# Four blocks of a depthwise convolution as ScalarE products and GpSimd sums, in place of three blocks as diagonal products on TensorE

## The chip, the cores and the metric

The kernel runs on one core of one Trainium2 chip. The metric is device microseconds of one execution, and the time given for a kernel is the median of its runs. Five engines take part: TensorE (PE in the rows, its weight loads PEld), VectorE (DVE), ScalarE (ACT), GpSimd (POOL) and SyncE (SP), which issues most DMAs. Each has its own queue of instructions, works through it in order, and waits on semaphores for the others.

## The reference, cut to what matters

Two transformer-like blocks over 256 tokens of width 2048 in float32. The first block starts with a mixer of two branches. One branch is a state-space model; the other is a convolution over time:

```python
def conformer_conv(a, w_dw, b_dw, ln_g, ln_b, w_pw):
    glu = a[..., :CONV_WIDTH] * jax.nn.sigmoid(a[..., CONV_WIDTH:])      # 1024 channels
    padded = jnp.pad(glu, ((0, 0), (CONV_KERNEL - 1, 0), (0, 0)))        # 31 taps
    y = lax.conv_general_dilated(padded, w_dw[:, None, :], ..., feature_group_count=CONV_WIDTH)
    y = y + b_dw
    y = jax.nn.silu(layernorm(y, ln_g, ln_b))
    return y @ w_pw
```

Every channel is convolved with its own 31 weights: y[c, t] = b[c] + sum over k of w[c, k] * glu[c, t + k - 30]. The rest of the model (the expert layer, a gated delta network and a banded attention) is not touched by the change.

## The kernel before

Activations lie with channels on the 128 partitions and the 256 tokens along the free axis, so 1024 channels are eight blocks of 128x256. A weight strip of 128x1024 float32 arrives by DMA (`raw`, line 150), ScalarE rounds it into a high part `wh` (line 162), VectorE subtracts to get the low part `wl` (line 163), and TensorE makes two products for each of its eight 128x128 pieces (`dual`, lines 175 and 176): the high part times the high and low halves of the activations (512 columns), the low part times the high half (256 columns). After 16 such pairs the two halves of the PSUM tile are folded together (ScalarE line 181, VectorE line 182), and VectorE scales the result into SBUF (`evict`, line 342).

While such products run, other work is woven between them. A `Side` holds generators; `mix` advances each of them by a fraction of a step after every pair, so a number in `STEP` is steps per block of 16 pairs. The instructions that a step traces on VectorE are held behind the last `wl` subtraction; what it traces on ScalarE and GpSimd is held by data, buffers and its place in the program alone. A scheduler fixes the order of each engine's queue when the kernel is built.

The convolution is made in the loop of line 415, which runs over the 32 blocks of the gates (blocks 24 to 55 of `w_in`) and in which three things are woven:

- `side`, the state-space scan, at 2 steps a block: VectorE products, additions and scans (lines 595 and 614 to 628), two GpSimd additions of 128x256 for every scan (lines 630 and 631), and TensorE products (lines 611, 612 and 639).
- `side2`, `conv` (line 665), blocks 0 to 4 of the convolution on VectorE, at 2.25 steps a block. A step is one tap of three blocks (0, 1, 2) and, after 31 steps, of two (3, 4): one `scalar_tensor_tensor` of 128x256 for each block and tap (line 674). That makes 62 steps.
- `side3`, `conv_pe` (line 704), blocks 5 to 7 on TensorE, at 3.7 steps a block. For each block, `glu` is split into high and low halves (line 722 on ScalarE, 723 on VectorE); for each tap ScalarE makes two 128x128 diagonal matrices from the identity (lines 728 and 729), in a ring of three, and TensorE multiplies with them by `dual`. After 31 taps the result is folded and moved to `cy` with its bias (line 718).

When `side3` has run out, the normalization `conv_norm` is put behind `conv` in the queue of `side2`. It sums all eight blocks of `cy` on TensorE (line 682). `glu`, `cy` and the weights `dw` are slices of the tile `cw`, and appear under that name in the rows.

Of the kernel before, what the change touches and what calls it, by code (L numbers as in the profile page):

```python
# [10 lines left out]
F32 = mybir.dt.float32  # L11
F32R = mybir.dt.float32r
# [4 lines left out]
AF = mybir.ActivationFunctionType  # L17
ALU = mybir.AluOpType
# [4 lines left out]
P = 128  # L23
W1 = 1024
W2 = 512
STEP = (6, 2, 2.25, 3.7, 3, 2)
GRATE = 0.2
DSTEP = 4.4
LAG = 7
# [8 lines left out]
GATE = 1024.0  # L38
GB = 8
GLAG = 2  # L40
CDVE = ((0, 1, 2), (3, 4))
CPE = (5, 6, 7)
DLAG = 2
TSTEP = 2
T = 256
KT = 16
# [70 lines left out]
class K:  # L117
# [189 lines left out]
    def mixers(self):  # L307
        nc, tc, I = self.nc, self.tc, self.I
        with ExitStack() as ctx:
            E = ctx.enter_context  # L310
            c1 = E(tc.tile_pool(name="c1", bufs=1))
# [5 lines left out]
            x = self.operand()  # L317
# [3 lines left out]
            o, w = VEC["mix"]  # L321
# [19 lines left out]
            def evict(dst, ps):  # L341
                nc.vector.tensor_tensor(out=dst, in0=ps, in1=rstd, op=ALU.mult)

            def block(n, between=None):
                ps = self.gemm([w_in[n, 0], w_in[n, 1]], x, between)
                return ps
# [34 lines left out]
            for j in range(3, 8):  # L381
                ps = block(16 + j, self.mix((side, STEP[5] / 16, "V")))
                evict(u[:, j, :], ps)

            glu = cw[:, 0:2288].rearrange("p (k t) -> p k t", k=8)
            cy = cw[:, 2304:4352].rearrange("p (k t) -> p k t", k=8)
            dw = cw[:, 4352:4600].rearrange("p (k t) -> p k t", k=8)
# [3 lines left out]
            for j in range(8):  # L391
                pa = block(j, self.mix((side, STEP[0] / 32, "V")))
                a = sm.tile([P, T], F32, name="ca")
                evict(a, pa)
                pg = block(8 + j, self.mix((side, STEP[0] / 32, "V")))
                g = sm.tile([P, T], F32, name="cg")
# [6 lines left out]
            side2 = Side()  # L403
            side2.add(self.conv(glu, cy, dw, CDVE))
            c4 = E(ExitStack())
            dg = c4.enter_context(tc.tile_pool(name="dg", bufs=DLAG + 1))
            side3 = Side()
            side3.add(self.conv_pe(c1, dg, glu, cy, dw, CPE))
            norm = self.conv_norm(sm, cy, *cx)
            bg = self.big_tile("bg")  # L410
            gt = bg.rearrange("p (k t) -> p k t", k=32)
# [3 lines left out]
            for j in range(32):  # L415
                ps = block(24 + j, self.mix((side, STEP[1] / 16, "V"), (side2, STEP[2] / 16, "V"), (side3, STEP[3] / 16, "V")))
                g = sm.tile([P, T], F32, name="gg")
# [11 lines left out]
            for j in range(16):  # L429
                ps = self.gemm([I["conv_w_out"][j, 0]], cx, self.mix((side, STEP[4] / 8, "V")))  # L430
                nc.vector.scalar_tensor_tensor(out=gt[:, j, :], in0=gt[:, j, :], scalar=1.0, in1=ps, op0=ALU.add, op1=ALU.mult)
# [33 lines left out]
            for j in range(16):  # L465
# [3 lines left out]
                ps = self.gemm([I["w_out"][j, 0], I["w_out"][j, 1]], mx)  # L469
# [231 lines left out]
            V.tensor_tensor(out=cl[:, j, :], in0=cy[:, j, :], in1=ch[:, j, :].bitcast(F32), op=ALU.subtract)  # L701
        yield

    def conv_pe(self, c1, dg, glu, cy, dw, js):

        nc = self.nc
        n = js[0]
        dh = c1.tile([P, len(js), 31], F32R, name="dwh")
        nc.scalar.copy(dh, dw[:, n:, :])
        dl = c1.tile([P, len(js), 31], F32, name="dwl")  # L710
        nc.vector.tensor_tensor(out=dl, in0=dw[:, n:, :], in1=dh.bitcast(F32), op=ALU.subtract)
        late = []

        def taps(ps, d, g, j, k):
            self.dual(ps, d[0], d[1], g[:, :, k : k + T], k == 0, k == 30)
            if k == 30:
                ps = self.fold(ps)
                nc.scalar.activation(cy[:, j, :], ps, AF.Identity, bias=self.vec("cb", j))

        for j in js:  # L720
            g = dg.tile([P, 2, 30 + T], F32R, name="g", bufs=1)
            nc.scalar.copy(g[:, 0], glu[:, j, :])
            nc.vector.tensor_tensor(out=g[:, 1], in0=glu[:, j, :], in1=g[:, 0].bitcast(F32), op=ALU.subtract)
            yield
            ps = self.ips.tile([P, 512], F32, name="cps", tag="i")
            for k in range(31):
                d = [dg.tile([P, P], F32R, name="d%d" % i) for i in range(2)]
                nc.scalar.activation(d[0], self.ident, AF.Copy, scale=dh.bitcast(F32)[:, j - n, k : k + 1])
                nc.scalar.activation(d[1], self.ident, AF.Copy, scale=dl[:, j - n, k : k + 1])
                late.append((ps, d, g, j, k))  # L730
                if len(late) > DLAG:
                    taps(*late.pop(0))
                yield
            while late:
                taps(*late.pop(0))
            yield


# [1027 lines left out]
```

## Time and profile before

| what | value |
|---|---|
| median of 3 runs | 3355.14 us (3352.12 to 3356.29) |
| the profiled execution | 3351.08 us |
| its span in the profile | 3349.3 us |
| mean granted clock of TensorE | 0.996 |
| TensorE busy | 3291.0 us (98%) |
| VectorE busy | 2667.1 us (80%) |
| ScalarE busy | 2021.3 us (60%) |
| GpSimd busy | 171.6 us (5%) |

Busy time is the union of the instructions' durations as recorded. A duration includes what the instruction waits for after it has been started; consecutive instructions of one engine overlap slightly, so the distance of two starts is shorter than a duration. Ends of matmuls are modelled. The loop of line 415 begins about 183 us after the start of the span; the sums of `conv_norm` begin at 409 us.

### The profile page before, as it was taken

How to read it: one execution, taken by the hardware profiler on the slowest of the kernel's cores; microseconds unless marked ns; L12 is line 12 of the kernel's file. 1: busy time of each engine (PE TensorE's matmuls, PEld its weight loads, DVE VectorE, ACT ScalarE, POOL GpSimd, SP SyncE). 2: the span in 40 equal slices, each digit the busy share in tenths (PEclk: the TensorE clock that was granted, in tenths of full speed). 3: DMA queues.
4: the chain of work that ended last, by engine and by line, in shares of the span. 5: the costliest groups of instructions: out<-in, count | busy, mean ns of one | idle time of the engine just before them, and what ended most of it. 6: DMA issues, size and time to landing. Idle time of an engine off the chain costs nothing.

```text
span 3349.3 us, 53879 instructions
## 1 busy us (share of the span) xinstructions
PE 3291.0 (98%) x17962; PEld 2780.5 (83%) x17962; DVE 2667.1 (80%) x6200; ACT 2021.3 (60%) x4529; POOL 171.6 (5%) x319
## 2 busy tenths in 40 slices
PE   8999999999999999999999999999999999999999
PEld 7787778888888888888888888778888888888888
DVE  8999987789999999996555556868888768666685
ACT  6577755555555555555555556767666666566664
POOL 1211110000000000000000000000222100000000
PEclk9999999999999999999999999999999999999999
DMA  6544345765556555555666666655443436655556
GB/s 210 160 143 139 133 127 188 216 193 178 187 183 179 180 177 182 177 182 183 193 194 195 193 192 198 209 183 171 143 138 117 145 105 211 198 177 176 173 171 181
DMA packets 167655, 584.49 MB, mean 175 GB/s; under 512 B 19184, under 2 KB 25616, under 8 KB 167120
## 3 DMA queue, kind: packets, MB, share of 16 engines
q1 hardware_dynamic: 165600, 574.94, 54.8%
q0 software_dynamic: 1776, 6.10, 0.6%
q8 instruction: 141, 2.31, 0.3%
q14 instruction: 138, 1.13, 0.1%
HBM read 573.88 MB, written 7.09 MB: 173 GB/s over the span
## 4 chain that ended last, share of the span: by engine, by line
PE 90%; DVE 5%; ACT 2%; issue 1%; DMA 1%; POOL 1%; SPq 0%; ACTq 0%; DVEq 0%; POOLq 0%
PE g L175 36%; PE g L176 18%; PE va L1018 7%; PE va L1019 7%; PE va L1020 7%; PE g L1609 3%; PE g L1610 3%; PE g L1608 3%; DVE wl L163 2%; PE ip L1345 1%; ACT wh L162 1%; PE yp L639 1%; PE wp L954 1%; PE cps L175 1%; PE bu L611 1%
## 5 line engine op out<-in xcount | busy, mean ns | idle before, releaser
L162 ACT CAST wh<-raw 128x512 fp32r<-128x512 f32 (+1 forms) x1920 | 1274.2, 664 | 1080.3 <-PE g L175 553.2
L163 DVE TENSOR_TENSOR wl<-raw,wh 128x512 fp32r<-128x512 f32 (+1 forms) x1920 | 1433.8, 748 | 589.6 <-ACT wh L162 571.8
L175 PE MATMUL g<-X,wh 128*128 128x512 f32 x4752 | 1707.7, 401 | 23.0 <-ACT wh L162 8.8
L176 PE MATMUL g<-X,wl 128*128 128x256 f32 x4752 | 1337.0, 281 | 2.3 <-DVE wl L163 2.2
L175 PEld LDWEIGHTS g<-X,wh 128*128 128x128 f32 x4752 | 894.3, 188 | 234.6 <-issue 10.8
L176 PEld LDWEIGHTS g<-X,wl 128*128 128x128 f32 x4752 | 898.0, 189 | 9.9 <-DVE wl L163 5.1
L1018 PE MATMUL va<-wh,ah 128*128 128x512 f32 x1024 | 398.4, 391 | 4.5 <-DVE gg L797 2.3
L1019 PE MATMUL va<-wh,al 128*128 128x512 f32 x1024 | 400.2, 391 | 0.3 <-DVE al L1010 0.3
L1020 PE MATMUL va<-wl,ah 128*128 128x512 f32 x1024 | 399.1, 390 | 0.0
L1018 PEld LDWEIGHTS va<-wh,ah 128*128 128x128 f32 x1024 | 191.7, 188 | 46.9 <-ACT ah L1009 7.5
L1019 PEld LDWEIGHTS va<-wh,al 128*128 128x128 f32 x1024 | 192.6, 188 | 43.3 <-DVE al L1010 3.3
L1020 PEld LDWEIGHTS va<-wl,ah 128*128 128x128 f32 x1024 | 192.7, 188 | 39.7
L175 PE MATMUL g<-xo,wh 128*128 128x512 f32 x512 | 179.6, 395 | 0.0
L182 DVE TENSOR_TENSOR g<-g,fold 128x256 f32<-128x256 f32 x377 | 159.8, 424 | 4.5 <-ACT fold L181 4.0
L1608 PE MATMUL g<-wh,X 128*128 128x512 f32 x384 | 151.9, 396 | 0.0
L1610 PE MATMUL g<-wl,X 128*128 128x512 f32 x384 | 150.5, 392 | 0.0
L1609 PE MATMUL g<-wh,X 128*128 128x512 f32 x384 | 150.1, 391 | 0.0
L181 ACT COPY fold<-g 128x256 f32<-128x256 f32 x377 | 138.2, 367 | 13.5 <-DVE g L182 7.7
L176 PE MATMUL g<-xo,wl 128*128 128x256 f32 x512 | 143.6, 280 | 0.0
L944 DVE TENSOR_SCALAR oj<-iota,ijg 128x128 f16<-128x128 f16 x512 | 142.6, 307 | 0.0
L175 PEld LDWEIGHTS g<-xo,wh 128*128 128x128 f32 x512 | 96.0, 187 | 22.8 <-DVE xo L1471 0.3
L1010 DVE TENSOR_TENSOR al<-w,ah 128x256 fp32r<-128x256 f32 x256 | 106.7, 418 | 0.9 <-ACT ah L1009 0.8
(478 smaller groups left out, 3577.0 us busy)
## 6 DMA issues: line engine op xcount, KB each, us to landing
raw<-peer_u SPq DMA_DIRECT2D x256, 512.0 KB, 3.5
raw<-peer_v SPq DMA_DIRECT2D x256, 512.0 KB, 3.5
raw<-a_w_in SPq DMA_DIRECT2D x128, 512.0 KB, 3.5
raw<-w_in SPq DMA_DIRECT2D x112, 512.0 KB, 3.5
raw<-b_w_t SPq DMA_DIRECT2D x96, 512.0 KB, 3.5
raw<-w_out SPq DMA_DIRECT2D x32, 512.0 KB, 4.3
raw<-peer_w_q SPq DMA_DIRECT2D x32, 512.0 KB, 3.5
raw<-a_w_out SPq DMA_DIRECT2D x32, 512.0 KB, 3.7
```

The source lines that it names most:

```text
L162: self.marks["A"] = nc.scalar.copy(wh[:, e], raw[:, e])
L163: self.marks["V"] = nc.vector.tensor_tensor(out=wl[:, e], in0=raw[:, e], in1=wh[:, e].bitcast(F32), op=ALU.subtract)
L175: nc.tensor.matmul(pf, lhsT=wh, rhs=hl, start=start, stop=False)
L176: return nc.tensor.matmul(pf[:, :T], lhsT=wl, rhs=hl[:, 0], start=False, stop=stop)
L182: self.nc.vector.tensor_tensor(out=pf[:, :T], in0=pf[:, :T], in1=t, op=ALU.add)
L944: V.tensor_scalar(out=oj[:, k, :], in0=iota, scalar1=ijg[:, 1, t : t + 1], scalar2=ijg[:, 2 + k, t : t + 1], op0=ALU.is_equal, op1=ALU.mult)
L1018: nc.tensor.matmul(ps, lhsT=ah, rhs=wh, start=first, stop=False)
L1019: nc.tensor.matmul(ps, lhsT=al, rhs=wh, start=False, stop=False)
L1020: nc.tensor.matmul(ps, lhsT=ah, rhs=wl, start=False, stop=last)
L1608: nc.tensor.matmul(ps[a], lhsT=xh[:, k, s], rhs=wh, start=k == 0, stop=False)
L1609: nc.tensor.matmul(ps[a], lhsT=xl[:, k, s], rhs=wh, start=False, stop=False)
L1610: self.marks["P"] = nc.tensor.matmul(ps[a], lhsT=xh[:, k, s], rhs=wl, start=False, stop=k == KT - 1)
```

## The change

Blocks 4 to 7 of the convolution go to ScalarE and GpSimd. For each tap ScalarE multiplies a shifted slice of `glu` by the tap's weights (128x256, one instruction a block), and GpSimd adds two blocks' products at once to `cy` (128x512). The first tap is written to `cy` directly, with the bias. VectorE keeps blocks 0 to 3, as two pairs. `conv_pe` and its pool are gone; the new pool `pr` holds three buffers of two blocks.

```diff
-STEP = (6, 2, 2.25, 3.7, 3, 2)
+STEP = (6, 2, 2.25, 1.4, 3, 2)
-CDVE = ((0, 1, 2), (3, 4))
-CPE = (5, 6, 7)
-DLAG = 2
+CDVE = ((0, 1), (2, 3))
+CADD = (4, 6, 8)
...
-            dg = c4.enter_context(tc.tile_pool(name="dg", bufs=DLAG + 1))
+            pr = c4.enter_context(tc.tile_pool(name="pr", bufs=3))
             side3 = Side()
-            side3.add(self.conv_pe(c1, dg, glu, cy, dw, CPE))
+            side3.add(self.conv_add(pr, glu, cy, dw, CADD))
...
-    def conv_pe(self, c1, dg, glu, cy, dw, js):
...
+    def conv_add(self, pr, glu, cy, dw, js):
 
         nc = self.nc
+        for k in range(31):
+            for a, b in zip(js, js[1:]):
+                t = None if k == 0 else pr.tile([P, b - a, T], F32, name="tap")
+                for j in range(a, b):
+                    x, w = glu[:, j, k : k + T], dw[:, j, k : k + 1]
+                    if k == 0:
+                        nc.scalar.activation(cy[:, j, :], x, AF.Identity, scale=w, bias=self.vec("cb", j))
+                    else:
+                        nc.scalar.activation(t[:, j - a, :], x, AF.Copy, scale=w)
+                if k:
+                    nc.gpsimd.tensor_tensor(out=cy[:, a:b, :], in0=cy[:, a:b, :], in1=t, op=ALU.add)
             yield
```

## Rows read from the trace of the kernel before

**Rows 1.** The page: busy time, share of the span and instructions of each engine, and the chain of work that ended last, by engine.

```profile
PE 3291.0 (98%) x17962; PEld 2780.5 (83%) x17962; DVE 2667.1 (80%) x6200; ACT 2021.3 (60%) x4529; POOL 171.6 (5%) x319
...
PE 90%; DVE 5%; ACT 2%; issue 1%; DMA 1%; POOL 1%; SPq 0%; ACTq 0%; DVEq 0%; POOLq 0%
```

**Rows 2.** Busy time of each engine in stretches of the convolution's stage. Columns: the stretch, its length, then busy time (and instructions) of PE, PEld, DVE, ACT and POOL, the granted clock, the share of the DMA engines, GB/s.

```profile
183.00:260.00 77.00, 77.00 (x423) 63.88 (x422) 76.06 (x138) 56.51 (x126) 7.45 (x8) 1.00 0.43 142
260.00:334.40 74.40, 71.94 (x387) 58.03 (x385) 72.70 (x130) 53.37 (x122) 9.78 (x10) 1.00 0.44 137
334.40:338.70 4.30, 0.00 (x0) 0.00 (x0) 4.30 (x9) 3.33 (x7) 0.00 (x0) 1.00 0.39 124
338.70:342.10 3.40, 3.40 (x8) 1.58 (x8) 3.40 (x9) 1.68 (x6) 0.00 (x0) 0.50 0.47 154
342.10:408.00 65.90, 65.90 (x361) 54.84 (x361) 63.65 (x115) 48.77 (x110) 8.50 (x10) 1.00 0.41 136
```

**Rows 3.** Groups of instructions by line in the stage, 183 to 408 us. Columns: line, engine, operation, out<-in, shapes, count | busy us, mean ns of one | idle time just before them and what ended it.

```profile
L175 PE MATMUL g<-X,wh 128*128 128x512 f32 x439 | 160.9, 402 | 1.8 <-ACT wh L162 1.0 <-DVE gg L342 0.8
...
L674 DVE SCALAR_TENSOR_TENSOR cw<-cw 128x256 f32<-128x256 f32 x150 | 73.9, 534 | 0.0
L163 DVE TENSOR_TENSOR wl<-raw,wh 128x1024 fp32r<-128x1024 f32 x54 | 68.4, 1266 | 4.9 <-ACT wh L162 4.7
...
L175 PE MATMUL cps<-g,d 128*128 128x512 f32 x93 | 37.1, 404 | 4.3 <-DVE g L723 4.3
L729 ACT ACTIVATE d<-ident,dwl 128x128 fp32r<-128x128 f32 x92 | 35.8, 389 | 0.0
L728 ACT ACTIVATE d<-ident,dwh 128x128 fp32r<-128x128 f32 x90 | 35.7, 397 | 33.8 <-PE cps L175 33.5
...
L182 DVE TENSOR_TENSOR g<-g,fold 128x256 f32<-128x256 f32 x27 | 11.3, 420 | 0.0
L342 DVE TENSOR_TENSOR gg<-g,rstd 128x256 f32<-128x256 f32 x27 | 11.1, 412 | 0.0
...
L718 ACT ACTIVATE cw<-cps,vecs 128x256 f32<-128x256 f32 x3 | 1.4, 471 | 0.0
L182 DVE TENSOR_TENSOR cps<-cps,fold 128x256 f32<-128x256 f32 x3 | 1.3, 421 | 0.0
...
L723 DVE TENSOR_TENSOR g<-cw,g 128x286 fp32r<-128x286 f32 x2 | 0.9, 442 | 0.0
```

**Rows 4.** Instructions of VectorE in order of time, around 375 us. Columns: start us, duration us (of all of them where a row has several), engine, line, operation, out<-in, shapes, count.

```profile
371.74 1.21 DVE L163 TENSOR_TENSOR wl<-raw,wh 128x1024 fp32r<-128x1024 f32 x1
...
373.54 0.86 DVE L674 SCALAR_TENSOR_TENSOR cw<-cw 128x256 f32<-128x256 f32 x2
...
375.27 1.83 DVE L674 SCALAR_TENSOR_TENSOR cw<-cw 128x256 f32<-128x256 f32 x2
...
380.07 0.47 DVE L674 SCALAR_TENSOR_TENSOR cw<-cw 128x256 f32<-128x256 f32 x1
```

**Rows 5.** Instructions of GpSimd in order of time, the same columns, with the idle time before the first of a pair in brackets.

```profile
192.74 0.74 POOL L630 TENSOR_TENSOR wk<-wk 128x256 f32<-128x256 f32 x1 [14.05 <-DVE wk L628]
193.43 0.74 POOL L631 TENSOR_TENSOR wk<-wk 128x256 f32<-128x256 f32 x1
...
313.95 1.99 POOL L630 TENSOR_TENSOR cw<-cw 128x256 f32<-128x256 f32 x1 [13.07 <-DVE cw L628]
...
375.09 0.86 POOL L630 TENSOR_TENSOR cw<-cw 128x256 f32<-128x256 f32 x1 [13.35 <-DVE cw L628]
375.91 0.92 POOL L631 TENSOR_TENSOR cw<-cw 128x256 f32<-128x256 f32 x1
```

**Rows 6.** A wider GpSimd product in a later stage of the kernel, and the VectorE instruction that ran into it; instructions in order of time.

```profile
2487.25 3.68 POOL L1337 TENSOR_TENSOR xx<-tab 128x2048 f32<-128x2048 f32 x1 [4.21 <-DVE wl L163]
...
2487.43 3.78 DVE L1250 SCALAR_TENSOR_TENSOR cy<-ci,dcw,cy 128x256 f32<-128x256 f32 x1
...
2491.47 0.47 DVE L1250 SCALAR_TENSOR_TENSOR cy<-ci,dcw,cy 128x256 f32<-128x256 f32 x1
```

**Rows 7.** Instructions of TensorE in order of time, around 365 and 371 us.

```profile
364.80 0.39 PE L175 MATMUL cps<-g,d 128*128 128x512 f32 x1
...
365.15 0.40 PE L175 MATMUL g<-X,wh 128*128 128x512 f32 x1
...
370.13 1.05 PE L639 MATMUL yp<-cw,sw 128*32 128x256 f32 x4
...
371.89 0.58 PE L175 MATMUL g<-X,wh 128*128 128x512 f32 x1
```

**Rows 8.** The products on ScalarE: eight scaled copies of 128x256 in a row, near the start of the kernel, in order of time.

```profile
11.57 3.31 ACT L485 ACTIVATE X<-bt,vecs 128x256 fp32r<-128x256 f32 x8
```

**Rows 9.** The instructions of the diagonal tile d over the whole kernel. Columns: line, engine, operation, out<-in, count: shortest/median/longest ns, first and last start us, shapes.

```profile
L728 ACT ACTIVATE d<-ident,dwh x93: 385/402/407, 49.8 to 393.5; 128x128 fp32r<-128x128 f32 x93
L729 ACT ACTIVATE d<-ident,dwl x93: 385/388/405, 182.2 to 393.8; 128x128 fp32r<-128x128 f32 x93
```

More of the change, by code (lines that the diff above doesn't have):

```diff
@@ L702, in conv_norm @@
         yield
-    def conv_pe(self, c1, dg, glu, cy, dw, js):
+    def conv_add(self, pr, glu, cy, dw, js):
         nc = self.nc
[L707 to L735, printed above, removed]
+        for k in range(31):
[9 more added lines that the diff above has]
+                    nc.gpsimd.tensor_tensor(out=cy[:, a:b, :], in0=cy[:, a:b, :], in1=t, op=ALU.add)
             yield
```

## The prediction

> **What bounds the kernel now.** I read the page first. Over the whole span TensorE is busy 98% of the time and the chain of work that ended last is 90% TensorE [rows 1], so a change that takes TensorE work away looks like a gain. But the change touches one stage only, about 225 us of 3349, and a share over the span says little about it. So I cut that stage into stretches [rows 2]. There VectorE is as full as TensorE: its busy times add up to 76.06 + 72.70 + 4.30 + 3.40 + 63.65 = 220.1 of 225.0 us. In the stretch from 334.4 to 338.7 us TensorE does nothing at all for 4.3 us and VectorE is busy through all of it.
>
> Which of the two is the limit can be counted. A pair of products takes 0.35 us from start to start, and the products of one scan 1.76 us (from 370.13 to 371.89) [rows 7]. The stage holds 439 pairs of the gates and 93 of the convolution [rows 3] and 14 scans (half of the 28 GpSimd additions [rows 2]): 532 x 0.35 + 14 x 1.76 = 211 us, 94% of 225. VectorE idles for 4.9 us, nearly all before a `wl` [rows 3]. So VectorE is the fuller of the two, and TensorE has some 14 us of room that its recorded busy time hides. Work taken from TensorE alone would be worth little here; what the change does to VectorE decides.
>
> **The change part by part.**
>
> *TensorE* loses 93 pairs, 93 x 0.35 = 32.6 us. It falls to about 178 us of work in the stage and is no limit any more. I count this at nothing: VectorE's work covers it.
>
> *VectorE* loses one of five convolution blocks, 31 instructions. Two in a row take 0.86 us and one 0.47 [rows 4], so one costs 0.39 us from start to start: 12.1 us. Three splits of `glu`, three folds and one small subtraction go too, 0.44 and 0.42 us each [rows 3], some 2.5 us. Together -14.6 us. Steps and their pace stay 62 and 2.25 a block, so `conv` still ends after 27.6 blocks and the normalization stays in its place in the program.
>
> *ScalarE* loses 186 diagonals (35.8 + 35.7 us busy [rows 3]) and about 3 us of casts, folds and moves. It gains 124 products. Eight scaled copies of 128x256 take 3.31 us [rows 8], 0.41 each; the move with bias, 0.47 [rows 3], bounds it above: 51 to 58 us. ScalarE gets emptier, from 164 us of 225 [rows 2] to some 145. Counted at nothing; its cover is the slack against VectorE, and what it costs if that fails is a rival below.
>
> *GpSimd* gains 60 additions of 128x512. The trace has none of that shape. One of 128x256 takes 0.74 us undisturbed [rows 5], a product of 128x2048 3.68 us [rows 6]; along that line 256 more columns cost (3.68 - 0.74) / 1792 x 256 = 0.42 us, so an addition takes 1.16 us, or at most twice 0.74. Sixty are 70 us plus waits, beside the 25.7 us that GpSimd does now [rows 2]. At 1.4 steps a block it ends after 22 blocks, before `conv`. It keeps up.
>
> *What the additions do to VectorE* is the term that decides. At 375.09 and 375.91 us GpSimd runs its two additions [rows 5]. At 375.27 VectorE starts two taps, which take 1.83 us in place of 0.86 [rows 4, 5]. Each addition has thus delayed a tap by 0.485 us, although no data connects them. The reverse shows too: an addition takes up to 1.99 us [rows 5] where 0.74 do. In the later stage a tap that starts just behind the 3.68 us product takes 3.78 us in place of 0.47 [rows 6]; the delay is 3.31 us, the GpSimd instruction's time less 0.37. So the two engines take turns, and a wider GpSimd instruction delays VectorE for longer. The folds and evictions keep means of 0.42 and 0.41 us [rows 3], so they pay nothing.
>
> How often the delay strikes is read from the stage. Taps have a mean of 0.534 us in place of 0.47, 150 of them: 9.6 us. `wl` has 1.266 in place of 1.21, 54 of them: 3.0 us [rows 3, 4]. That is 12.6 us for 28 additions, 0.45 each, 93% of 0.485: VectorE nearly always wants what GpSimd holds.
>
> For 128x512 the delay lies on the line from 0.485 (256 columns) to 3.31 (2048): 0.485 + 2.83 / 1792 x 256 = 0.89 us. Below it is bounded by 0.485, as if width cost nothing; above by twice that, 0.97. I take 0.89, since the two measured widths fix the slope, and a share of 0.9, a little less because the longer hold leaves more room for a fold or an eviction to pass. 60 x 0.89 x 0.9 = 48 us; the ends are 60 x 0.485 x 0.9 = 26 and 60 x 0.97 = 58 us.
>
> A rule bears on this. The Trainium skill, SBUF — State Buffer, section "SBUF: two separate sides", says that VectorE and GpSimd share a pair of SBUF ports under an exclusive lock, that a VectorE instruction with two SBUF inputs needs it, and that the loser blocks for the whole of the other's instruction. By that, a whole addition would be lost each time, 60 x 1.16 x 0.9 = 63 us; the rows show 0.25 to 0.37 us less per instruction, and I go by the rows. The same skill, GPSIMD Engine Reference, section "Engine selection", advises VectorE for elementwise additions because GpSimd is about two times slower; the row agrees (0.74 against 0.42 us at 128x256).
>
> *Sum:* 48 - 14.6 = +33 us on the engine that limits the stage, whether the additions keep the pace of 1.4 or run ahead: their number is the same. The profiled execution took 3351.1 us, so 3384. The three runs have a median of 3355.1, 4 us above it; I predict 3386, between the two.
>
> **The rivals.**
>
> *The additions fall where VectorE does not mind* (faster). The place is the same stage; the mechanism is that additions run beside folds, evictions and scan products with a PSUM input, or while VectorE waits. Then only the -14.6 us is left, 3338 us. It decides below a mean delay of 14.6 / 60 = 0.24 us an addition. Against it stands 0.45 us as now measured for additions half as wide, and that the undisturbed additions at 192.74 us [rows 5] are rare. 8%.
>
> *Nearly even*: width costs nothing and some additions hide in VectorE's 4.9 us of idle time [rows 3]. 60 x 0.485 x 0.9 - 14.6 - 4.9 = +7 us, 3358 to 3362. 6%.
>
> *ScalarE's queue stalls, and `wh` comes late* (slower still). A product needs one of three buffers, which an addition must free. While it waits, the casts to `wh` behind it on ScalarE wait, behind them `wl` on VectorE, and behind it TensorE. That products are put far ahead of their place is seen: the first diagonals ran at 49.8 us, long before the loop [rows 9], and diagonals waited 33.5 us for their ring [rows 3]. If in each of 30 steps VectorE stands for half of an addition and a tap's wait behind it, 30 x 0.7 = 21 us more: 3405. TensorE, with 178 us of work in some 258, will have gaps; after the gap of 4.3 us its clock was 0.50 for 3.4 us [rows 2], the lower of the two levels. Each such spell costs at most 1.7 us of TensorE's time, for which it has room; ten that hit the path add 17 us, to the same end. 22%.
>
> *The change does not do what it says*: GpSimd ends last and the normalization's sums wait for it. An addition would have to take 258 / 60 = 4.3 us with its waits; the longest now is 1.99 [rows 5]. 2%, with about +40 us or more.
>
> **How the numbers follow.** The forecast has 62%, with its own range of +11 (26 - 14.6) to +44 (58 - 14.6), 3362 to 3397 from the two bases. The range of 8 in 10 leaves out the faster rival at its lower end and takes in the stall at its upper: 3362 to 3414. Below 3362 lie the faster and most of the even case; above 3414 the worse stalls. About 0.2%, 6.7 us, is what a measurement of this kernel can tell from no change. Faster by more than that 8%, within it 6%, slower 86%.
>
> **What would show it.** In the changed profile's same stage: TensorE with visible gaps and VectorE full; line 674 with 124 taps whose mean is well over 0.534 us, many near 1.36 (0.47 + 0.89), and `wl` over 1.266 us; folds and evictions unchanged at 0.42 and 0.41; 60 GpSimd additions of 1.2 to 2 us; the sums of the normalization beginning at about 442 us in place of 409, and from there on the same distances. The prediction is wrong if taps keep means near 0.5 us while the additions run, if a 128x512 addition takes far from 1.2 us undisturbed, or if VectorE shows idle time before `wl` that grows with ScalarE's waits for the products' buffers: then the stall, not the shared turn, sets the time. It is also wrong if the stage gets shorter, which would say that TensorE had been the limit after all.

## The result, and the profile after

The changed kernel takes 3396.65 us (median; 3394.1 to 3399.88), the kernel before in the same comparison 3353.8 us: 1.28% slower, ratio 1.0128 with a 95% interval of 1.011 to 1.0145. The forecast was 3386 us, within 3362 to 3414. Direction, stage and mechanism were right; the loss was 43 us where the sum said 33.

The page of the changed kernel, busy time by engine (line numbers after the change are one lower than before: 673 is the tap that was 674, 162 the `wl` that was 163, 341 and 181 the eviction and the fold; 714 is the new product on ScalarE, 716 the new addition on GpSimd):

```profile
span 3392.3 us, 53518 instructions
...
PE 3280.1 (97%) x17776; PEld 2761.7 (81%) x17776; DVE 2709.7 (80%) x6162; ACT 2012.8 (59%) x4457; POOL 273.8 (8%) x379
```

Against [rows 1], TensorE and ScalarE are a little emptier, GpSimd has 102 us more, and VectorE, which lost work, is busy for 43 us longer: as much as the span grew. Where that lies is seen in the stage. Busy time of each engine in stretches of the changed kernel's stage, columns as in [rows 2], the last row the whole stage:

```profile
220.00:260.00 40.00, 29.48 (x141) 22.21 (x140) 40.00 (x46) 25.82 (x54) 28.68 (x19) 0.93 0.33 105
260.00:300.00 40.00, 31.39 (x138) 23.51 (x138) 38.89 (x47) 25.83 (x54) 26.73 (x19) 0.85 0.32 99
300.00:340.00 40.00, 25.91 (x122) 20.61 (x122) 39.19 (x47) 24.41 (x50) 24.83 (x18) 0.91 0.32 99
340.00:455.00 115.00, 101.20 (x512) 78.67 (x511) 109.00 (x186) 55.84 (x92) 18.06 (x17) 0.97 0.43 138
183.00:455.00 272.00, 218.55 (x1054) 168.91 (x1052) 263.31 (x367) 156.38 (x297) 121.46 (x85) 0.93 0.38 120
```

The stage, up to the last tap, has grown from 225 to 272 us. While the additions run (the last starts at 339 us), VectorE is busy nearly all the time and yet finishes only 46 or 47 instructions in 40 us; afterwards it finishes 186 in 115 us. TensorE stands for a fifth to a third of the first part, with a granted clock between 0.85 and 0.93. The groups of the changed kernel, 183 to 455 us, to be held against [rows 3]:

```profile
L716 POOL TENSOR_TENSOR cw<-cw,tap 128x512 f32<-128x512 f32 x57 | 91.5, 1627 | 46.7 <-ACT tap L714 46.6
L673 DVE SCALAR_TENSOR_TENSOR cw<-cw 128x256 f32<-128x256 f32 x119 | 84.6, 745 | 0.0
L162 DVE TENSOR_TENSOR wl<-raw,wh 128x1024 fp32r<-128x1024 f32 x59 | 81.0, 1372 | 8.7 <-ACT wh L161 8.5
...
L714 ACT ACTIVATE tap<-cw 128x256 f32<-128x256 f32 x111 | 49.6, 499 | 5.9 <-POOL cw L716 5.9
...
L181 DVE TENSOR_TENSOR g<-g,fold 128x256 f32<-128x256 f32 x28 | 11.8, 421 | 0.0
L341 DVE TENSOR_TENSOR gg<-g,rstd 128x256 f32<-128x256 f32 x27 | 11.2, 415 | 0.0
```

There are 31 taps fewer on VectorE, and together they take longer: a mean of 0.745 us in place of 0.534. `wl` rose from 1.266 to 1.372 us. The fold and the eviction, each with one input in PSUM, are as before. The shortest additions show what one takes undisturbed, 1.27 us (shortest, median and longest in ns, first and last start in us):

```profile
L716 POOL TENSOR_TENSOR cw<-cw,tap x60: 1266/1477/2266, 159.1 to 339.1; 128x512 f32<-128x512 f32 x60
```

One tap in order of time, VectorE first and then GpSimd (as [rows 4, 5]):

```profile
212.53 0.47 DVE L673 SCALAR_TENSOR_TENSOR cw<-cw 128x256 f32<-128x256 f32 x1
213.77 1.23 DVE L162 TENSOR_TENSOR wl<-raw,wh 128x1024 fp32r<-128x1024 f32 x1 [0.77 <-ACT wh L161]
214.91 1.51 DVE L673 SCALAR_TENSOR_TENSOR cw<-cw 128x256 f32<-128x256 f32 x1
```

```profile
214.29 1.85 POOL L716 TENSOR_TENSOR cw<-cw,tap 128x512 f32<-128x512 f32 x1 [5.40 <-ACT tap L714]
```

The addition is started while `wl` runs, waits for it and is done at 216.14 us. The tap started at 214.91 waits for the addition and takes 1.51 us in place of 0.47: a delay of 1.04 us.

To add this up I took for every VectorE instruction how much longer it was than its like usually is in the kernel before (the quarter point of the durations of its shape: a quarter of them are shorter). From 145 us to the end of the convolution this excess is 15.1 us before and 69.7 us after; the experiments below are counted in the same way.

These two stretches do not hold the same work, since the longer one takes in more strips of the gates. So the sum is made from the start of the program's 41st `wl` (145.7 us before, 147.5 after) to that of its 121st (477.8 and 522.3), between which every kernel here passes the same 80 strips. VectorE's work is its instructions taken at their usual distances from start to start; all values in us:

| kernel | length | VectorE's work | excess | VectorE idle |
|---|---|---|---|---|
| before | 332.1 | 299.0 | 16.4 | 15.7 |
| changed | 374.9 | 284.3 | 73.9 | 16.7 |
| no additions (experiment 1) | 327.0 | 284.3 | 22.8 | 19.3 |
| memsets (experiment 6) | 324.2 | 284.3 | 22.4 | 17.2 |

The work fell by 14.7 us, the excess rose by 57.5 and the idle time by 1.0: 43.8 us, where the stretch grew by 42.7.

### The profile page after: what moved, and what is told of

Read it like the earlier page. It is cut to its first block, busy times and chain, and to the rows that moved or that the text cites. A ratio compares the mean times of both kernels' runs of the same rounds, so it can differ in the third digit from the quotient of the medians.

```text
span 3392.3 us, 53518 instructions
## 1 busy us (share of the span) xinstructions
PE 3280.1 (97%) x17776; PEld 2761.7 (81%) x17776; DVE 2709.7 (80%) x6162; ACT 2012.8 (59%) x4457; POOL 273.8 (8%) x379
## 5 line engine op out<-in xcount | busy, mean ns | idle before, releaser
L175 PEld LDWEIGHTS g<-X,wl 128*128 128x128 f32 x4752 | 904.3, 190 | 32.3 <-DVE wl L162 24.5
L180 ACT COPY fold<-g 128x256 f32<-128x256 f32 x377 | 138.6, 368 | 41.8 <-DVE g L181 36.2
```

Of the source, the lines that this page charges most:

```text
L175: return nc.tensor.matmul(pf[:, :T], lhsT=wl, rhs=hl[:, 0], start=False, stop=stop)
```

## The experiments

Theory: GpSimd and VectorE take turns, and each addition costs VectorE most of its own length. Rivals: ScalarE's new products stall its queue; TensorE's gaps and lower clock reach the path; running ahead is what hurts. Where nothing else is said, the rows below are groups of instructions by line of the kernel of that experiment, from 183 to 455 us, with columns as in [rows 3].

**1. No additions.**

```diff
-                if k:
+                if k == 30:
                     nc.gpsimd.tensor_tensor(out=cy[:, a:b, :], in0=cy[:, a:b, :], in1=t, op=ALU.add)
```

> The changed kernel with 58 of the 60 GpSimd additions left out (only the last tap is added), so blocks 4 to 7 of the convolution are incomplete; all products on ScalarE stay. If GpSimd and VectorE take turns and that is the loss, about 58 delays of 0.9 us go: 3397 - 52 = 3345 us, faster than before by the VectorE work that the change saved (some 10 us). If the products on ScalarE or TensorE's lower clock are the loss, little changes: above 3375 us.

Measured: 3349.67 us, ratio to before 0.9979 (0.9969 to 0.9988). The taps and `wl` of this kernel:

```profile
L162 DVE TENSOR_TENSOR wl<-raw,wh 128x1024 fp32r<-128x1024 f32 x68 | 84.8, 1249 | 12.2 <-ACT wh L161 11.9
L673 DVE SCALAR_TENSOR_TENSOR cw<-cw 128x256 f32<-128x256 f32 x120 | 62.9, 558 | 0.0
```

With all 120 products still on ScalarE the taps are back at 0.558 us and the loss is gone, so the products are not its cause. The excess is 18.8 us; 58 additions account for the other 50.9, 0.88 us each. The kernel is only 6 us faster than before in this comparison, not 10. By the table, 6.4 of the 14.7 us of saved work come back as longer instructions and 3.5 as idle time, nearly all of it waiting for `wh`. The two additions that are left explain less than 2 us of the 6.4, and experiments 2, 6 and 10, which have none, also show 6 us more excess than before. About 4 of the 6 are the scan's own GpSimd additions: over the 80 strips the VectorE instructions that ran beside them are 14.2 us longer than usual before and 17.6 to 19.1 in these four kernels, with 34 to 36 delayed by over 0.3 us in place of 26. Why more are struck was not followed up.

**2. The additions on VectorE.**

```diff
-                    nc.gpsimd.tensor_tensor(out=cy[:, a:b, :], in0=cy[:, a:b, :], in1=t, op=ALU.add)
+                    nc.vector.tensor_tensor(out=cy[:, a:b, :], in0=cy[:, a:b, :], in1=t, op=ALU.add)
```

> The changed kernel with the same 60 additions of 128x512 on VectorE in place of GpSimd. Turns: an addition costs VectorE 0.60 us from start to start itself, where it now loses about 0.91 us to GpSimd's: 60 x 0.31 = 19 us faster than the changed kernel, 3378 us, although VectorE has 36 us more to do. If GpSimd's additions run beside VectorE at little cost and ScalarE's stalls are the loss, VectorE's 36 us come on top, less some 20 us of stalls: 3412 us.

Measured: 3385.1 us, ratio 1.0089 (1.0072 to 1.0106); 11.5 us faster than the changed kernel, by less than the 19 expected. The taps of this kernel and its additions, now on VectorE:

```profile
L673 DVE SCALAR_TENSOR_TENSOR cw<-cw 128x256 f32<-128x256 f32 x120 | 62.0, 550 | 0.0
...
L716 DVE TENSOR_TENSOR cw<-cw,tap 128x512 f32<-128x512 f32 x60 | 40.1, 698 | 0.0
```

VectorE does the additions itself, 36 us more work, and the kernel is faster: what GpSimd took from VectorE was more than what it did for it. That is the plainest verdict of the study.

**3. The additions at their pace.**

```diff
-... (side3, STEP[3] / 16, "V")))
+... (side3, STEP[3] / 16, "AV")))
```

> The changed kernel with the products on ScalarE held behind the last cast to wh, as their place in the program says, so that products and additions no longer run ahead (they now end at 339 us, about 16 blocks after the start). Turns: the number of additions is the same, 3397 us within 6. If crowded additions, ScalarE's stalls or TensorE's lower clock (47.6 us of it between 183 and 560 us) are a part of the loss, the spread-out version is faster by 15 to 20 us: about 3380 us.

Measured: 3397.32 us, ratio 1.0128 (1.0111 to 1.0145), the same as the changed kernel. The additions now start between 184 and 389 us in place of 159 and 339, and the excess is 68.2 us in place of 69.7. Running ahead as far as the changed kernel does costs nothing, and fewer of them at a time gain nothing: the number counts.

**4. No products.**

```diff
-                t = None if k == 0 else pr.tile([P, b - a, T], F32, name="tap")
+                if k == 1 and a == js[0]:
+                    t = pr.tile([P, b - a, T], F32, name="tap", bufs=1)
...
-                    else:
+                    elif k == 1 and a == js[0]:
                         nc.scalar.activation(t[:, j - a, :], x, AF.Copy, scale=w)
```

> The changed kernel with 118 of the 120 products of the later taps left out; every addition reads the one product tile that is made, so blocks 4 to 7 are not computed. 60 additions stay. Turns: the same delays, 3397 us within 8. If the products on ScalarE (a wait for a free buffer, casts to wh behind it) are a part of the loss: some 20 us faster, 3377 us.

Measured: 3406.62 us, ratio 1.0151 (1.0134 to 1.0168), 10 us slower than the changed kernel; neither theory had this. The excess is 71.1 us, as before, so the additions cost the same. Freed of the products they run nearly back to back, from 159 to 266 us, 26 of the 60 while the blocks of `glu` are still made, the last of which starts 19 us later than in the changed kernel (205.6 against 186.8 us). VectorE's idle time is 18.9 us in place of 9.9, which is about the difference. Most of the growth is one wait of 8.29 us, and the trace shows where it comes from:

```profile
251.90 1.74 DVE L627 TENSOR_TENSOR cw<-cw,wk 128x512 f32<-128x512 f32 x1
257.04 9.33 POOL L717 TENSOR_TENSOR cw<-cw,tap 128x512 f32<-128x512 f32 x6
266.33 0.90 POOL L629 TENSOR_TENSOR cw<-cw 128x256 f32<-128x256 f32 x1
267.29 1.91 PE L638 MATMUL yp<-cw,sw 128*32 128x256 f32 x4 [17.14 <-POOL cw L629]
273.85 1.05 ACT L161 CAST wh<-raw 128x1024 fp32r<-128x1024 f32 x1 [22.24 <-PE g L174]
274.94 1.23 DVE L162 TENSOR_TENSOR wl<-raw,wh 128x1024 fp32r<-128x1024 f32 x1 [8.29 <-ACT wh L161]
```

The scan's own GpSimd addition (line 629) had its input at 253.64 us and stood behind the new additions in GpSimd's queue until 266.33. TensorE waited 17 us for it, `wh` for TensorE, and `wl` for `wh`. So additions that run far enough ahead do cost something, by way of GpSimd's queue. The stall theory, by which the time falls without products, is wrong.

**5. Narrow additions.**

```diff
-CADD = (4, 6, 8)
+CADD = (4, 5, 6, 7, 8)
...
-            pr = c4.enter_context(tc.tile_pool(name="pr", bufs=3))
+            pr = c4.enter_context(tc.tile_pool(name="pr", bufs=6))
```

> The changed kernel with its additions cut in two: 120 GpSimd additions of 128x256, each of one block, in six buffers of one block. If the loss grows with the columns added, as the line through 0.485 us (256 columns) and 3.31 us (2048) says, 120 x 0.485 x 0.9 = 52 us are lost in place of about 55: 3394 us, within 6. If it is a loss for each instruction, it doubles: about 3440 us. If VectorE loses little by such additions: no more than 3380 us.

Measured: 3385.75 us, ratio 1.0089 (1.0074 to 1.0105), below the 3394 +- 6 that a loss by columns gave. This kernel's additions and taps, and the additions' shortest, median and longest:

```profile
L716 POOL TENSOR_TENSOR cw<-cw,tap 128x256 f32<-128x256 f32 x117 | 121.1, 1068 | 17.4 <-ACT tap L714 17.2
L673 DVE SCALAR_TENSOR_TENSOR cw<-cw 128x256 f32<-128x256 f32 x120 | 83.3, 728 | 0.0
L716 POOL TENSOR_TENSOR cw<-cw,tap x120: 721/919/1811, 145.6 to 336.8; 128x256 f32<-128x256 f32 x120
```

Twice the instructions cost less, not more: 61.6 us of excess, less some 17 that remain without additions (18.8 in experiment 1, which still has two of them): 45 us for 120, 0.37 each. A tap that is hit takes 0.95 us here, as in [rows 4]. So the loss goes by columns, and somewhat under it for short instructions: 0.37 of the 0.485 us that a hit costs is a share of 76%, where the wide ones have 85%. That short ones more often fall beside an instruction that doesn't wait would explain it; it wasn't tested.

**6. A memset in place of the addition.**

```diff
-                    nc.gpsimd.tensor_tensor(out=cy[:, a:b, :], in0=cy[:, a:b, :], in1=t, op=ALU.add)
+                    nc.gpsimd.memset(cy[:, a:b, :], 0.5)
```

> The changed kernel with a GpSimd memset of the same 128x512 slice of cy in place of each addition, so blocks 4 to 7 are not computed. A memset reads nothing. If VectorE waits for any GpSimd instruction, 60 of these cost about 0.4 us each (a memset of 128x2048 takes 1.79 us in the trace of before): 3345 + 20 = 3365 us. If it waits only for one that reads SBUF, nothing is lost: 3349 us, like the run without additions. The Trainium skill, SBUF — State Buffer, section "SBUF: two separate sides", says the latter.

Measured: 3345.75 us, ratio 0.9974 (0.9964 to 0.9984). This kernel's taps and memsets (half of the memsets ran before 183 us):

```profile
L673 DVE SCALAR_TENSOR_TENSOR cw<-cw 128x256 f32<-128x256 f32 x120 | 63.9, 567 | 0.0
L716 POOL MEMSET cw<- 128x512 f32 x30 | 16.0, 533 | 6.5 <-ACT cw L712 4.9
```

Sixty GpSimd instructions of 0.53 us that write and don't read cost VectorE nothing that shows: the 66 VectorE instructions that ran beside one are together 1.5 us longer than usual, where in the changed kernel the 123 beside an addition are 57.0 us longer. Being busy is not what matters; reading is, and experiment 11 tests the other side of it.

**7. The scan's two additions on VectorE**, in the kernel before.

```diff
-            nc.gpsimd.tensor_tensor(out=t1[:, 0, :], in0=t1[:, 0, :], in1=t2[:, 1, :], op=ALU.subtract)
-            nc.gpsimd.tensor_tensor(out=t1[:, 1, :], in0=t1[:, 1, :], in1=t2[:, 0, :], op=ALU.add)
+            V.tensor_tensor(out=t1[:, 0, :], in0=t1[:, 0, :], in1=t2[:, 1, :], op=ALU.subtract)
+            V.tensor_tensor(out=t1[:, 1, :], in0=t1[:, 1, :], in1=t2[:, 0, :], op=ALU.add)
```

> The kernel before with the scan's two additions of 128x256 on VectorE in place of GpSimd (64 in all, 28 in the stage of the convolution). Turns: each costs VectorE 0.33 us itself and now loses it 0.45: 28 x 0.12 = 3 us in the stage, up to 7 us over all scans: 3349 us, 0.1 to 0.2% faster. If GpSimd's additions were free for VectorE: 64 x 0.33 = 21 us slower at most, 3377 us.

Measured: 3366.77 us, ratio 1.0044 (1.003 to 1.0057): slower, where 0.1 to 0.2% faster was expected. The excess from 40 to 510 us fell from 22 to 8 us, so the 64 additions had cost 14 us, 0.22 each, half of what I had read off the pairs that hit; doing them costs 0.33 each, 21 us. In the stage of the convolution alone, over the same 54 strips, the excess fell from 13.8 to 4.6 us: 0.33 for each of its 28 additions, where the prediction had read 0.45. The slowdown is more than 21 - 14 us; VectorE's idle time over the 80 strips also rose, by 6.6 us. Over all scans, many of the additions meet no VectorE instruction that waits. For these narrow and sparse additions GpSimd is the better place.

**8. Four blocks on TensorE**, in the kernel before.

```diff
-STEP = (6, 2, 2.25, 3.7, 3, 2)
+STEP = (6, 2, 2.25, 4.8, 3, 2)
-CDVE = ((0, 1, 2), (3, 4))
-CPE = (5, 6, 7)
+CDVE = ((0, 1), (2, 3))
+CPE = (4, 5, 6, 7)
```

> The kernel before with blocks 4 to 7 as diagonal products on TensorE (31 taps more there, at 4.8 steps a block) and blocks 0 to 3 on VectorE; no GpSimd addition. VectorE loses 12.1 us of taps, TensorE gains 31 x 0.35 = 10.9 us and stands at 222 of the stage's 225 us. With VectorE as the limit before: up to 3 us faster, 3350 us; if TensorE had been the limit all along: 3366 us.

Measured: 3356.05 us, ratio 0.9999 (0.999 to 1.0008), the same as before. Busy time by engine in three stretches of this kernel's stage, columns as in [rows 2]:

```profile
183.00:260.00 77.00, 77.00 (x422) 63.85 (x422) 74.20 (x135) 62.82 (x154) 12.17 (x10) 1.00 0.44 139
260.00:340.00 80.00, 80.00 (x440) 66.39 (x439) 71.91 (x132) 66.94 (x159) 11.08 (x10) 1.00 0.42 135
340.00:405.00 65.00, 65.00 (x358) 54.01 (x357) 58.58 (x106) 52.91 (x125) 8.50 (x8) 1.00 0.43 138
```

Now TensorE has no gap at all and VectorE has 17 us of idle time in 222 us. The limit has changed sides and the time is the same, where up to 3 us less was expected: before the change the two engines were nearly in balance. That VectorE was ahead of TensorE is not shown by this run.

**9. Half of the additions.**

```diff
-CDVE = ((0, 1), (2, 3))
-CADD = (4, 6, 8)
+CDVE = ((0, 1, 2), (3, 4, 5))
+CADD = (6, 8)
```

> The changed kernel with half of the additions: blocks 0 to 5 on VectorE (two groups of three), blocks 6 and 7 by ScalarE and 30 GpSimd additions of 128x512. Counted by the runs so far, an addition costs VectorE 0.88 us ((69.7 - 18.8) / 58, the excess of its durations with and without 58 of the additions) and a tap 0.39: 30 x 0.88 less and 62 x 0.39 more than the changed kernel, -26 + 24 = 3394 us, within 6. If the loss grows faster than the number of additions: below 3385 us.

Measured: 3404.97 us, ratio 1.0137 (1.012 to 1.0154), outside the 3394 +- 6. The excess is 44.2 us, 25.5 less than with 60 additions, so the 26 for 30 additions are confirmed; the 62 taps more come to 24.5 us. What was not counted is VectorE's idle time, 21.2 us in place of 9.9. Two waits of this kernel, 145 to 480 us (total, times, longest), and one stretch of its stage, columns as in [rows 2]:

```profile
DVE wl L162 <- ACT wh L161: 21.6, 25, 2.2
ACT wh L161 <- PE g L174: 101.9, 49, 8.1
260.00:300.00 40.00, 32.15 (x137) 24.72 (x136) 35.39 (x65) 16.04 (x27) 4.60 (x5) 0.81 0.37 116
```

The idle time is `wl` waiting for `wh` (21.6 us in 25 waits; in the changed kernel 10.1 in 13), and `wh` waits for TensorE, whose granted clock here was 0.81. So TensorE's clock may well reach the path in this kernel; how much of the idle time it makes was not tested.

**10. Everything on VectorE.**

```diff
-CDVE = ((0, 1), (2, 3))
-CADD = (4, 6, 8)
+CDVE = ((0, 1, 2, 3), (4, 5, 6, 7))
+CADD = (8,)
```

> The changed kernel with no addition: all eight blocks on VectorE, in two groups of four; neither TensorE, ScalarE nor GpSimd takes part in the convolution. 60 additions less and 124 taps more: 3397 - 53 + 48 = 3392 us, as good as the changed kernel or better, which would say that GpSimd's help takes from VectorE more than the whole work it spares. If GpSimd's additions are a real relief for VectorE: 3397 + 48 - 30 = 3415 us or more.

Measured: 3395.41 us, ratio 1.012 (1.0103 to 1.0137); the changed kernel has 3396.65. This kernel's taps:

```profile
L673 DVE SCALAR_TENSOR_TENSOR cw<-cw 128x256 f32<-128x256 f32 x240 | 111.7, 523 | 0.0
```

VectorE alone makes all 248 taps in the time in which it makes 124 of them with ScalarE's and GpSimd's help. For VectorE an addition of two blocks on GpSimd (0.88 us) costs about what two taps do (0.78).

**11. A copy in place of the addition.**

```diff
-                    nc.gpsimd.tensor_tensor(out=cy[:, a:b, :], in0=cy[:, a:b, :], in1=t, op=ALU.add)
+                    nc.gpsimd.tensor_copy(cy[:, a:b, :], t)
```

> The changed kernel with a GpSimd copy of the product tile to cy (one input, 128x512) in place of each addition, so blocks 4 to 7 are not summed. The memset, which read nothing, cost nothing (3345.8 us). If one read input is enough to make VectorE wait, 60 copies of some 0.6 us cost about 0.4 each: 3346 + 25 = 3371 us. If only two inputs do: 3346 us.

Measured: 3360.7 us, ratio 1.0013 (1.0003 to 1.0022), 15 us over the memset. This kernel's taps and copies:

```profile
L673 DVE SCALAR_TENSOR_TENSOR cw<-cw 128x256 f32<-128x256 f32 x120 | 68.9, 609 | 0.0
L716 POOL COPY cw<-tap 128x512 f32<-128x512 f32 x57 | 53.1, 953 | 48.8 <-ACT tap L714 48.6
```

One read input is enough to make VectorE wait. The copy takes 0.61 us undisturbed, half of the addition, and its excess over the memset's is 33.0 - 18.2 = 14.8 us, 0.25 each, in place of the 0.4 expected. The instructions that are hit wait some 0.4 us; fewer are hit than was counted on.

**12. Wide additions.**

```diff
-CADD = (4, 6, 8)
+CADD = (4, 8)
...
-            pr = c4.enter_context(tc.tile_pool(name="pr", bufs=3))
+            pr = c4.enter_context(tc.tile_pool(name="pr", bufs=1))
```

> The changed kernel with 30 GpSimd additions of 128x1024 (all four blocks at once) and one buffer of four blocks in place of three of two. The undisturbed additions took 0.72 us (256 columns) and 1.27 (512), so 1024 take 2.35 and delay a tap by 2.1: 30 x 2.1 x 0.86 = 54 us, as 60 of 512 do: 3397 us within 8. If the loss per column falls with width as the product of 128x2048 suggested (3.31 us for 2048): 30 x 1.70 x 0.86 = 44 us, 3388 us. If the single buffer makes ScalarE and GpSimd wait for one another and that reaches VectorE: over 3410 us.

Measured: 3400.25 us, ratio 1.0133 (1.0117 to 1.015), within the 3397 +- 8 of the first case. This kernel's taps, additions and products, the additions' shortest, median and longest, and a tap that is hit:

```profile
L673 DVE SCALAR_TENSOR_TENSOR cw<-cw 128x256 f32<-128x256 f32 x118 | 87.6, 778 | 0.0
...
L716 POOL TENSOR_TENSOR cw<-cw,tap 128x1024 f32<-128x1024 f32 x30 | 78.4, 2614 | 80.6 <-ACT tap L714 80.6
L714 ACT ACTIVATE tap<-cw 128x256 f32<-128x256 f32 x117 | 53.8, 500 | 41.9 <-POOL cw L716 41.8
...
L716 POOL TENSOR_TENSOR cw<-cw,tap x30: 2339/2548/3484, 185.3 to 378.9; 128x1024 f32<-128x1024 f32 x30
...
244.61 2.60 DVE L673 SCALAR_TENSOR_TENSOR cw<-cw 128x256 f32<-128x256 f32 x1
```

The additions take 2.34 us undisturbed and the taps that are hit 2.6, a delay of 2.1 us. ScalarE stands 41.8 us for the one buffer, and still the time is within 4 us of the changed kernel's: ScalarE's queue has that room. No version among these beats the kernel before with the whole convolution computed.

## Why the prediction was right, and where its size was off

*VectorE as the limit of the stage*: right for the changed kernel, but for the kernel before by less than the text made of it. Experiment 8 relieved VectorE by one block, TensorE became the limit at once, and the time stayed. Of the 14 us of room that I gave TensorE it used 10.9, and these were there.

*VectorE's own work*, -14.6 us: measured -14.7. It could not be had in full: without additions 6.4 us came back as longer instructions and 3.5 as waiting, and the kernel was 6 us faster, or 10 with memsets (in two comparisons), not 15. So the price of the faster rival (3338 us) was too low by 8 to 12 us. *TensorE at nothing*: right here, although its gaps brought the clock to 0.85 in one stretch; VectorE's idle time rose by 1.0 us. *ScalarE at nothing*: right within the 3.5 us of waiting in experiment 1; without the products experiment 4 was not faster, and with one buffer experiment 12 was 4 us slower. A product took 0.50 us, and 0.40 from start to start.

*The turns*: right in mechanism; experiments 1, 2, 6 and 11 show that VectorE's taps wait for GpSimd instructions that read. The term was mis-sized: 60 x 0.89 x 0.9 = 48 us, where the excess rose by 57.5. The step that failed is the line through [rows 6]. The wide product there is a multiplication whose operands are repeated along the row, and it takes 3.68 us for 2048 columns; additions of ordinary operands take 0.72, 1.27 and 2.34 us for 256, 512 and 1024, about 2.1 ns a column where the line had 1.64. Whether the operation or the repeated operands make the difference was not tested. So an addition took 1.27 us and not 1.16, and the tap it hit waited 1.03 to 1.04 us and not 0.89, over even my upper bound of 0.97, which had doubled the short one's delay. The additions came to 60 x 0.88 = 53 us.

The share, 0.9, was nearly right: 0.88 / 1.03 = 0.85. That is in part luck. It was read from the scan's additions as 93%, and experiment 7 shows that these cost 0.33 us each in the stage, 68% of 0.485; part of the longer means that I put down to them stays when they are gone.

Of the 10 us between +33 and +43, 5 are the mis-sized delay. Some 5 are longer instructions that the kernels without the new additions show too, for the most part because the scan's additions strike more often; the sum did not have them. The idle time adds 1.

*The additions keep pace, and the pace doesn't matter*: right for the changed kernel; they ran ahead, the last started at 339 us, and experiment 3 gave the same time at the slower pace. Experiment 4 shows that it stops being right when they run further ahead. *The range's upper part*, kept for ScalarE's stalls and the clock, was needed for neither; the result, 3396.65 us, lies just under 3397, the upper end of the forecast's own range, because of the mis-sized term.

The Trainium skill's rule on the shared ports (SBUF — State Buffer, "SBUF: two separate sides") holds in what it says of reading: the memset cost nothing and the copy did. That a whole instruction is lost would have given 63 us by the length I used, and 60 x 1.27 x 0.85 = 65 us by the measured one; the runs show 0.24 us less at a hit, and 53 in all.

## What to carry to other kernels

Before work is moved to an engine that stands idle, look at what the busy engine's instructions do beside that engine's in the present trace: two VectorE taps of 1.83 us in place of 0.86 told the outcome. An addition moved to GpSimd pays only if it takes from VectorE less than VectorE would need for it; here 128x512 cost 0.88 us against 0.60, while the scan's 128x256 cost 0.22 against 0.33. Price an unseen size by rows of the same operation on the same kind of operands, not by the nearest shape alone. And when two versions are compared by stretches of their traces, let the stretches hold the same work.

## What was not expected of the hardware

- GpSimd additions of ordinary operands cost 2.1 ns a column (0.72, 1.27 and 2.34 us for 256, 512 and 1024 columns), a multiplication with repeated operands takes 3.68 us for 2048, where 2.1 a column would make 4.3.
- The delay of a VectorE tap is the GpSimd instruction's undisturbed time less some 0.24 us at all three widths: 0.485 of 0.72, 1.03 of 1.27, 2.1 of 2.34.
- A GpSimd memset of 128x512 (0.53 us) delays VectorE by nothing, a copy of it (0.61 us) by 0.25 us on average, although it reads one input only.
- 42 us of waits on ScalarE for one buffer (experiment 12, 4 us slower than the changed kernel), and a TensorE clock of 0.85 to 0.93 over 120 us (the changed kernel, VectorE's idle time up by 1.0 us), left hardly a mark on the time of a stage that VectorE sets.
- GpSimd's queue can hold up the other engines: a scan's addition that was ready at 253.64 us started at 266.33 behind the new ones, and TensorE waited 17 us (experiment 4).
